# RWKV-7 chunk outputs: products with the state first and together, products with R in a row, one PSUM clear per half

## The chip, the cores and the metric

The kernel runs on one core of one Trainium2 chip. The metric is the device time of one execution in microseconds, as a median over runs. The engines are TensorE (PE, matrix products; PEld is its weight load), VectorE (DVE), ScalarE (ACT), GpSimd (POOL) and SyncE (SP, which issues most of the transfers). Each engine works through its own instruction stream in order and waits for the others by semaphores.

## What is computed

One step of a one-layer decoder over 1024 prompt tokens and 8 x 4 sample tokens: a norm, one input projection, two groups of token mixers (8 RWKV-7 heads of 64, 4 HGRN2 heads of 128), one output projection, a squared-ReLU MLP and a final norm. The change is in the RWKV part, whose reference is a scan over the tokens:

```python
def step(s, inp):
    r_t, w_t, k_t, v_t, kk_t, a_t = inp
    sa = jnp.einsum('bhvk,bhk->bhv', s, -kk_t)
    s = (s * w_t[:, :, None, :] + sa[..., None] * (kk_t * a_t)[:, :, None, :]
         + v_t[..., None] * k_t[:, :, None, :])
    o = jnp.einsum('bhvk,bhk->bhv', s, r_t)
    return s, o
```

Each head has a state s of 64 x 64. The output o of a token comes from the state ahead of a chunk of tokens and from what the tokens of the chunk itself have added.

## The kernel before

The kernel has two stages. In the first, `mixers`, TensorE runs the input projection (`gemm`, lines L208 to L210, three fp32r products of 128 x 128 weights with 256 columns each, `ps_in`) quarter by quarter of the tokens, and between its products the small products of HGRN2, of RWKV, and of the adaLN conditioning (L240, L241, `ps_adp`). The second stage is the output projection and the MLP (`ps_g`, L1137).

RWKV takes the prompt in 8 groups of 128 tokens, each group in two chunks of 64, so 16 chunks one behind another; the samples are a group of their own with their own function. `rwkv_chain` does the chunks. The eight heads lie as four pairs j; the half h of a pair lies on partitions 0 to 63 or 64 to 127 (`hs`). A chunk goes through these steps, with `st` the state ahead of the chunk:

- `ps_U` (L928): for each half four products of `ar` with the state, 64 rows by 64 columns; VectorE adds W (L929).
- `ps_SA` (L933): eight products of the inverse XT with U, 64 by 64; ScalarE copies the result into R (L934).
- `ps_S` (L940): eight products of `btm` with R over 128 rows, halves in turn; VectorE makes the new state of it (L946, L947).
- `ps_O`: for each j and half one product of `ar` with the state (L953, 64 rows) and one of `Ar` with R (L954, 128 rows), both into the same columns of one PSUM tile. ScalarE copies it (L963 in `rwkv_centre`), and VectorE takes the mean and the variance.

The first chunk has no state and leaves out `ps_U` and L953. An fp32 product stands as two records in the trace, so eight products are 16 records. The tag of `ps_O` has one PSUM buffer, which it shares with `ps_oT`, the transposed output of a finished group.

The order on each engine isn't that of the code: a planner with a time model orders the instructions by their dependencies and by the priority in which the generators in `mixers` give them out. So one edit here can move instructions of other functions.

Of the kernel before, what the change touches and what calls it, by code (L numbers as in the profile page):

```python
# [7 lines left out]
F32 = mybir.dt.float32  # L8
# [6 lines left out]
P = 128  # L15
# [68 lines left out]
PT = "maso"  # L84
# [71 lines left out]
class Kernel:  # L156
# [751 lines left out]
    def rwkv_chain(self, g, pool, pp):  # L908

        nc = self.nc  # L910
        V, G, S = nc.vector, nc.gpsimd, nc.scalar
        g["oc"] = pool.tile([P, g["nch"], 4, 64], F32, tag="oc", name="oc", bufs=B_oc)
        g["var"] = pool.tile([P, g["nch"], 4], F32, tag="var", name="var", bufs=B_var)
        W, XT, ar = g["W"], g["XT"], g["ar"]
        for c in range(g["nch"]):
            st = self.rst
            hb = 1 - (c & 1)
            bs = slice(hb * 64, hb * 64 + 64)
            Ar, bt, R = g["Ar"][c], g["bt_"][c], g["R"][c]
            if st is None:  # L920
                U = W
            else:
                U = pool.tile([P, 2, 4, 64], F32, tag="U", name="U", bufs=B_U)
                for h in range(2):
                    hs = slice(h * 64, h * 64 + 64)
                    ps = pp.tile([P, 4, 64], F32, tag=PT[2], name="ps_U")
                    for j in range(4):
                        nc.tensor.matmul(ps[bs, j, :], lhsT=ar[hs, j, c, 0, :], rhs=st[hs, j, :], start=True, stop=True)  # L928
                    V.tensor_tensor(U[bs, h], ps[bs], W[bs, h], op=ALU.add)  # L929
            ps = pp.tile([P, 4, 2, 64], F32, tag=PT[2], name="ps_SA")  # L930
            for h in range(2):
                for j in range(4):
                    nc.tensor.matmul(ps[bs, j, h, :], lhsT=XT[bs, h * 4 + j, :], rhs=U[bs, h, j, :], start=True, stop=True)  # L933
            S.activation(R[bs], ps[bs], AF.Copy)  # L934
            yield
            ps = pp.tile([P, 4, 64], F32, tag=PT[2], name="ps_S")
            for j in range(4):
                for h in range(2):
                    hs = slice(h * 64, h * 64 + 64)
                    nc.tensor.matmul(ps[hs, j, :], lhsT=bt[:, j, hs], rhs=R[:, j, h, :], start=True, stop=True)  # L940
            sn = pool.tile([P, 4, 64], F32, tag="st", name="st", bufs=B_st)
            ptb = g["pt"][:, :, c:c + 1].to_broadcast([P, 4, 64])
            if st is None:
                V.tensor_tensor(sn, ps, ptb, op=ALU.mult)
            else:
                V.tensor_tensor(sn, ps, st, op=ALU.add)  # L946
                V.tensor_tensor(sn, sn, ptb, op=ALU.mult)  # L947
            ps = pp.tile([P, 4, 64], F32, tag=PT[3], name="ps_O")
            for j in range(4):
                for h in range(2):  # L950
                    hs = slice(h * 64, h * 64 + 64)
                    if st is not None:
                        nc.tensor.matmul(ps[hs, j, :], lhsT=ar[hs, j, c, 1, :], rhs=st[hs, j, :], start=True, stop=False)  # L953
                    nc.tensor.matmul(ps[hs, j, :], lhsT=Ar[:, h, j, :], rhs=R[:, j, h, :], start=st is None, stop=True)  # L954
            self.rwkv_centre(pool, g, c, ps)
            self.rst = sn
            yield

# [910 lines left out]
```

## Time and profile before

| | |
|---|---|
| median of 3 runs | 1934.76 us (1928.95 to 1952.22) |
| profiled execution | 1959.38 us |
| its span | 1957.6 us |
| TensorE busy | 1793.7 us, 92% |
| VectorE busy | 1175.9 us, 60% |
| GpSimd busy | 994.3 us, 51% |
| ScalarE busy | 919.0 us, 47% |

The profiled execution is 24.6 us longer than the median. Times within the span are counted from its start. A row of the timeline gives start, length, engine, line, operation, output and inputs, shapes and the number of records; records of one kind behind one another are merged into a row. A matmul's length runs to its modelled end, so that consecutive matmuls overlap, and what one costs is read from start to start. The granted clock of TensorE has two levels in these rows, 1.00 (2.4 GHz) and 0.50 (1.2 GHz).

### The profile page before, as it was taken

How to read it: one execution, taken by the hardware profiler on the slowest of the kernel's cores; microseconds unless marked ns; L12 is line 12 of the kernel's file. 1: busy time of each engine (PE TensorE's matmuls, PEld its weight loads, DVE VectorE, ACT ScalarE, POOL GpSimd, SP SyncE). 2: the span in 40 equal slices, each digit the busy share in tenths (PEclk: the TensorE clock that was granted, in tenths of full speed). 3: DMA queues.
4: the chain of work that ended last, by engine and by line, in shares of the span. 5: the costliest groups of instructions: out<-in, count | busy, mean ns of one | idle time of the engine just before them, and what ended most of it. 6: DMA issues, size and time to landing. Idle time of an engine off the chain costs nothing. (4 is left out here: it accounts for less than half of the span.)

```text
span 1957.6 us, 38042 instructions
## 1 busy us (share of the span) xinstructions
PE 1793.7 (92%) x13988; PEld 1646.0 (84%) x13988; DVE 1175.9 (60%) x2286; ACT 919.0 (47%) x1915; POOL 994.3 (51%) x1418
## 2 busy tenths in 40 slices
PE   6889889899899999999999799699999999999795
PEld 3778778767788888888888799699999899999795
DVE  7676834534744534565544456853333768799998
ACT  5455343653534455555463454545455454333332
POOL 4766362363617233336263566764544637264564
PEclk9998899867679878888796899899999999999896
DMA  7876578645558775635352743353333431423022
GB/s 264 280 235 192 174 237 262 196 125 138 146 154 262 232 230 157 195 117 175 114 160 64 250 170 104 107 167 117 98 99 125 145 132 53 136 75 127 19 76 89
DMA packets 219593, 303.33 MB, mean 155 GB/s; under 512 B 48616, under 2 KB 111464, under 8 KB 216336
## 3 DMA queue, kind: packets, MB, share of 16 engines
q1 hardware_dynamic: 199232, 275.74, 44.6%
q10 hardware_dynamic: 20080, 25.11, 3.8%
q8 instruction: 110, 1.80, 0.4%
q14 instruction: 75, 0.61, 0.1%
q0 software_dynamic: 96, 0.07, 0.0%
HBM read 237.17 MB, written 61.44 MB: 153 GB/s over the span
## 5 line engine op out<-in xcount | busy, mean ns | idle before, releaser
L1137 PE MATMUL ps_g<-bh,whi 128*128 128x264 f32 x1792 | 377.6, 291 | 51.1 <-DVE acc L1449 15.6
L1137 PE MATMUL ps_g<-bh,wlo 128*128 128x264 f32 x1792 | 374.3, 290 | 3.2 <-DVE wlo L1126 3.2
L1137 PE MATMUL ps_g<-bl,whi 128*128 128x264 f32 x1792 | 376.3, 290 | 0.7 <-DVE bl L1426 0.6
L1137 PEld LDWEIGHTS ps_g<-bh,whi 128*128 128x128 f32 x1792 | 287.7, 193 | 55.2 <-ACT whi L1125 16.3
L210 PE MATMUL ps_in<-h,wlo 128*128 128x256 f32 (+1 forms) x960 | 299.0, 313 | 10.0 <-POOL wlo L199 5.6
L208 PE MATMUL ps_in<-h,whi 128*128 128x256 f32 (+1 forms) x960 | 301.1, 318 | 5.7 <-ACT h L1090 3.5
L209 PE MATMUL ps_in<-l,whi 128*128 128x256 f32 (+1 forms) x960 | 298.3, 311 | 3.4 <-DVE l L1091 3.3
L1137 PEld LDWEIGHTS ps_g<-bh,wlo 128*128 128x128 f32 x1792 | 286.0, 193 | 3.8 <-DVE wlo L1126 3.8
L1137 PEld LDWEIGHTS ps_g<-bl,whi 128*128 128x128 f32 x1792 | 287.4, 194 | 1.3 <-DVE bl L1426 1.3
L195 ACT ACTIVATE whi<-wraw 128x512 fp32r<-128x512 f32 x240 | 149.5, 628 | 183.3 <-PE ps_in L209 122.4
L210 PEld LDWEIGHTS ps_in<-h,wlo 128*128 128x128 f32 x960 | 200.1, 209 | 23.1 <-POOL wlo L199 7.9
L208 PEld LDWEIGHTS ps_in<-h,whi 128*128 128x128 f32 x960 | 200.0, 210 | 14.7 <-issue 4.6
L209 PEld LDWEIGHTS ps_in<-l,whi 128*128 128x128 f32 x960 | 200.9, 209 | 10.1 <-DVE l L1091 4.3
L1125 ACT ACTIVATE whi<-wd 128x512 fp32r<-128x512 f32 x112 | 70.1, 630 | 184.2 <-PE ps_g L1137 152.8
L238 POOL TENSOR_TENSOR walo<-wada,wahi 128x256 fp32r<-128x256 f32 x128 | 95.9, 762 | 97.6 <-ACT wahi L237 88.3
L1126 POOL TENSOR_TENSOR wlo<-wu,whi 128x512 fp32r<-128x512 f32 x64 | 90.2, 1412 | 83.4 <-ACT whi L1125 83.2
L1125 ACT ACTIVATE whi<-wu 128x512 fp32r<-128x512 f32 x112 | 69.3, 628 | 119.6 <-PE ps_g L1137 111.0
L1426 POOL TENSOR_TENSOR bl<-u,bh 128x528 fp32r<-128x528 f32 x34 | 63.1, 1862 | 87.9 <-ACT bh L1425 77.8
L862 POOL TENSOR_TENSOR itmp<-ixt,iat 128x60 f32<-128x60 f32 (+24 forms) x248 | 76.1, 307 | 36.0 <-DMA iat<-at_d 17.6
L1426 DVE TENSOR_TENSOR bl<-u,bh 128x528 fp32r<-128x528 f32 x78 | 88.5, 1163 | 5.4 <-ACT bh L1425 5.3
L1126 DVE TENSOR_TENSOR wlo<-wd,whi 128x512 fp32r<-128x512 f32 x91 | 82.7, 913 | 12.3 <-ACT whi L1125 12.3
L864 POOL TENSOR_TENSOR ixt<-ixt,itmp 128x60 f32<-128x60 f32 (+24 forms) x248 | 78.1, 315 | 15.3
(426 smaller groups left out, 3910.7 us busy)
## 6 DMA issues: line engine op xcount, KB each, us to landing
wraw<-w_in SPq DMA_DIRECT2D x240, 256.0 KB, 4.1
wlo<-wlo_d SPq DMA_DIRECT2D x180, 256.0 KB, 3.9
wu<-w_up SPq DMA_DIRECT2D x74, 256.0 KB, 3.0
u<-u_d SPq DMA_DIRECT2D x16, 1056.0 KB, 4.9
wada<-w_ada SPq DMA_DIRECT2D x64, 256.0 KB, 3.8
wd<-w_down SPq DMA_DIRECT2D x64, 256.0 KB, 2.7
wlo_d<-wlo SPq DMA_DIRECT2D x60, 256.0 KB, 3.3
u_d<-c SPq DMA_DIRECT2D x48, 264.0 KB, 3.4
```

Source lines behind the costliest of these rows:

```text
L195: nc.scalar.activation(hi, raw, AF.Copy)
L208: nc.tensor.matmul(out, lhsT=wh, rhs=ah, start=first and k == 0, stop=False)
L209: nc.tensor.matmul(out, lhsT=wh, rhs=al, start=False, stop=False)
L210: nc.tensor.matmul(out, lhsT=wl, rhs=ah, start=False, stop=last and k == len(w) - 1)
L238: (nc.vector if k in ADV else nc.gpsimd).tensor_tensor(lo, raw[:, :, k, :], hi.bitcast(F32), op=ALU.subtract)
L862: G.tensor_tensor(tm, xt[:, 0:ns, j:j + 1].to_broadcast([P, ns, w]), at[:, j, j + 1:32].unsqueeze(1).to_broadcast([P, ns, w]), op=ALU.mult)
L864: G.tensor_tensor(dst, dst, tm, op=ALU.add)
L1125: self.nc.scalar.activation(hi, src, AF.Copy)
L1126: eng.tensor_tensor(lo, src, hi.bitcast(F32), op=ALU.subtract)
L1137: nc.tensor.matmul(out[c], lhsT=w[x][:, k, :], rhs=a[y][:, k, c * 264:c * 264 + 264], start=first and k == 0 and j == 0, stop=last and k = ...
L1426: F().tensor_tensor(lo[:, k, :], src[:, k, :], hi[:, k, :].bitcast(F32), op=ALU.subtract)
```

## The change

The tile of `ps_O` is taken before `ps_SA`, and the eight products with the state are written there in a row, j by j with the halves in turn. The eight products with R follow `ps_S` in a row. Before, each product with the state began a sum of its own (start set) and the one with R closed it. Now only the first product of each half (j = 0) has start set, which clears that half of the PSUM bank; the other products add or overwrite. The number of products, their operands and their shapes are unchanged. `ps_U` and `ps_S` only get another form of loop.

```diff
+        halves = (slice(0, 64), slice(64, 128))
...
+            po = pp.tile([P, 4, 64], F32, tag=PT[3], name="ps_O")
+            if st is not None:
+                for j in range(4):
+                    for hs in halves:
+                        nc.tensor.matmul(po[hs, j, :], lhsT=ar[hs, j, c, 1, :], rhs=st[hs, j, :], start=j == 0, stop=False, skip_group_check=True)
             ps = pp.tile([P, 4, 2, 64], F32, tag=PT[2], name="ps_SA")
...
-            ps = pp.tile([P, 4, 64], F32, tag=PT[3], name="ps_O")
             for j in range(4):
-                for h in range(2):
-                    hs = slice(h * 64, h * 64 + 64)
-                    if st is not None:
-                        nc.tensor.matmul(ps[hs, j, :], lhsT=ar[hs, j, c, 1, :], rhs=st[hs, j, :], start=True, stop=False)
-                    nc.tensor.matmul(ps[hs, j, :], lhsT=Ar[:, h, j, :], rhs=R[:, j, h, :], start=st is None, stop=True)
-            self.rwkv_centre(pool, g, c, ps)
+                for h, hs in enumerate(halves):
+                    nc.tensor.matmul(po[hs, j, :], lhsT=Ar[:, h, j, :], rhs=R[:, j, h, :], start=st is None and j == 0, stop=j == 3, skip_group_check=True)
+            self.rwkv_centre(pool, g, c, po)
```

On TensorE, at the first half of `ps_U` in the second chunk, there stood before one product with the state ahead of the projection:

```order
L904 MATMUL ps_x_3569<-XT,xt_3400 32x32 x8
L928 MATMUL ps_U<-st,ar 64x64 x4
L953 MATMUL ps_O<-st,ar 64x64
L210 MATMUL ps_in<-h_3482,wlo 128x256
L208 MATMUL ps_in<-h_3484,whi 128x256
```

Now all eight stand there (L935 is the new line of the product with the state):

```order
L904 MATMUL ps_x_3569<-XT,xt_3400 32x32 x8
L928 MATMUL ps_U<-st,ar 64x64 x4
L935 MATMUL ps_O<-st,ar 64x64 x8
L210 MATMUL ps_in<-h_3482,wlo 128x256
L208 MATMUL ps_in<-h_3484,whi 128x256
```

At the end of the same chunk on TensorE, products with R and with the state alternated; the rows go on in this way to the eighth product with R:

```order
L241 MATMUL ps_adp<-walo,c_hl 9x256
L940 MATMUL ps_S<-R,btm 64x64 x8
L954 MATMUL ps_O<-R,Ar 64x64
L953 MATMUL ps_O<-st,ar 64x64
L954 MATMUL ps_O<-R,Ar 64x64
```

Now the eight products with R (new line L955) follow those of `ps_S` (now L945), which have the same shape:

```order
L240 MATMUL ps_adp<-wahi,c_hl 18x256
L945 MATMUL ps_S<-R,btm 64x64 x8
L955 MATMUL ps_O<-R,Ar 64x64 x8
L793 MATMUL ps_A<-ar,bk 128x128 x4
L241 MATMUL ps_adp<-walo,c_hl 9x256
```

Of the 15 chunks with a state, eleven now have the eight products with the state in one piece; the others have them in two to eight pieces. In the stream of TensorE two neighbours differ in shape (rows or columns of the array used) 860 times before and 691 times now; of these 257 and 68 have a product of `ps_O` as one of the two. On all engines the instructions ahead of the second chunk and those of the second stage stand as before.

## Rows read from the trace of the kernel before

**Rows 1.** The page: TensorE busy and its granted clock, tenths in 40 slices.

```profile
PE   6889889899899999999999799699999999999795
PEclk9998899867679878888796899899999999999896
```

**Rows 2.** Busy time by engine in seven stretches, 440 to 1090 us: their sum.

```profile
sum 650.00, PE 624.04 PEld 541.25 DVE 323.36 ACT 314.13 POOL 279.01; mean PE 89.15 PEld 77.32 DVE 46.19 ACT 44.88 POOL 39.86
```

**Rows 3.** Groups of TensorE, 440 to 1090 us: busy us, mean ns, idle before.

```profile
L954 PE MATMUL ps_O<-R,Ar 128*64 128x64 f32 x256 | 42.3, 257 | 0.0
L953 PE MATMUL ps_O<-st,ar 64*64 64x64 f32 x240 | 42.0, 259 | 0.9 <-DVE hss L508 0.9
```

**Rows 4.** Timeline of TensorE, second chunk: start us, length us, instruction, records.

```profile
453.49 0.28 PE L953 MATMUL ps_O<-st,ar 64*64 64x64 f32 x2
453.70 0.39 PE L210 MATMUL ps_in<-h,wlo 128*128 128x256 f32 x1
...
465.94 0.28 PE L954 MATMUL ps_O<-R,Ar 128*64 128x64 f32 x2
466.15 0.33 PE L953 MATMUL ps_O<-st,ar 64*64 64x64 f32 x2
...
469.74 1.68 PE L793 MATMUL ps_A<-ar,bk 64*128 64x128 f32 x8
```

**Rows 5.** Timeline of TensorE, a chunk at half clock.

```profile
1035.04 1.96 PE L933 MATMUL ps_SA<-U,XT 64*64 64x64 f32 x16
1036.93 1.11 PE L467 MATMUL ps_l<-hz 128*128 128x64 f32 x4
...
1040.43 1.12 PE L940 MATMUL ps_S<-R,btm 128*64 128x64 f32 x16
1041.34 0.42 PE L954 MATMUL ps_O<-R,Ar 128*64 128x64 f32 x2
...
1047.33 1.06 PE L896 MATMUL ps_x<-ident,XT 32*32 32x32 f32 x16
```

**Rows 6.** Timeline of TensorE: the first chunk's rows, and a ps_SA at full clock.

```profile
450.29 0.69 PE L940 MATMUL ps_S<-R,btm 128*64 128x64 f32 x16
450.80 0.64 PE L954 MATMUL ps_O<-R,Ar 128*64 128x64 f32 x16
451.37 1.06 PE L577 MATMUL ps_os<-hs,hqs 128*32 128x128 f32 x8
...
1015.18 1.14 PE L933 MATMUL ps_SA<-U,XT 64*64 64x64 f32 x16
1016.25 0.49 PE L497 MATMUL ps_o<-hst,hqe 128*128 128x128 f32 x2
```

**Rows 7.** Busy time by stretch: nine at half clock behind alternations, first, last, sum.

```profile
470.20:497.50 27.30, 24.07 (x116) 19.96 (x115) 18.96 (x61) 6.46 (x17) 10.04 (x26) 0.50 0.59 161
...
1071.00:1077.70 6.70, 6.70 (x40) 5.32 (x41) 1.85 (x5) 2.25 (x6) 1.70 (x3) 0.50 0.01 2
sum 139.10, PE 135.88 PEld 116.76 DVE 67.80 ACT 47.10 POOL 36.25; mean PE 15.10 PEld 12.97 DVE 7.53 ACT 5.23 POOL 4.03
```

Behind the stretch stand its length, the busy time of PE, PEld, DVE, ACT and POOL with their instructions, the granted clock, the DMA share and GB/s.

**Rows 8.** The same view of two other stretches.

```profile
569.20:627.20 58.00, 58.00 (x548) 48.95 (x546) 25.61 (x59) 27.20 (x66) 37.95 (x95) 1.00 0.83 258
...
716.00:746.60 30.60, 30.20 (x192) 25.05 (x193) 11.85 (x28) 12.32 (x25) 19.65 (x50) 0.50 0.34 104
```

**Rows 9.** Timeline of TensorE: the projection at full clock and at half clock.

```profile
454.04 0.28 PE L209 MATMUL ps_in<-l,whi 128*128 128x256 f32 x1
454.16 0.28 PE L210 MATMUL ps_in<-h,wlo 128*128 128x256 f32 x1
...
883.51 0.42 PE L208 MATMUL ps_in<-h,whi 128*128 128x256 f32 x1
883.72 0.41 PE L209 MATMUL ps_in<-l,whi 128*128 128x256 f32 x1
```

**Rows 10.** Waits, 440 to 1090 us: us in total, times, longest.

```profile
ACT o L963 <- PE ps_O L954: 43.3, 13, 7.4
```

More of the change, by code (lines that the diff above doesn't have):

```diff
@@ L937, in rwkv_chain @@
             for j in range(4):
-                for h in range(2):
-                    hs = slice(h * 64, h * 64 + 64)
+                for h, hs in enumerate(halves):
                     nc.tensor.matmul(ps[hs, j, :], lhsT=bt[:, j, hs], rhs=R[:, j, h, :], start=True, stop=True)
@@ L947, in rwkv_chain @@
                 V.tensor_tensor(sn, sn, ptb, op=ALU.mult)
-            ps = pp.tile([P, 4, 64], F32, tag=PT[3], name="ps_O")
             for j in range(4):
-                for h in range(2):
-                    hs = slice(h * 64, h * 64 + 64)
-                    if st is not None:
-                        nc.tensor.matmul(ps[hs, j, :], lhsT=ar[hs, j, c, 1, :], rhs=st[hs, j, :], start=True, stop=False)
-                    nc.tensor.matmul(ps[hs, j, :], lhsT=Ar[:, h, j, :], rhs=R[:, j, h, :], start=st is None, stop=True)
-            self.rwkv_centre(pool, g, c, ps)
+                for h, hs in enumerate(halves):
+                    nc.tensor.matmul(po[hs, j, :], lhsT=Ar[:, h, j, :], rhs=R[:, j, h, :], start=st is None and j == 0, stop=j == 3, skip_group_check=True)
+            self.rwkv_centre(pool, g, c, po)
             self.rst = sn
```

## Prediction

> **What bounds the kernel now.** I read the page's busy slices first, then the stretch in which the edited lines run, then TensorE's instructions in order of time, and last the granted clock around them. TensorE is busy in nearly every slice of the span and its clock is below full in many slices of the middle [rows 1]. The edited lines run between about 451 and 1083 us. There the stretches of 440 to 1090 us give TensorE 624.04 us of 650.00, 96%; VectorE has 323.36, ScalarE 314.13, GpSimd 279.01 [rows 2]. So in this stage the in-order instruction stream of TensorE sets the pace: what it no longer does ends the stage earlier, until another engine's waits appear. Before 451 us and after some 1095 us the instructions and their order are the same in both kernels, so nothing is forecast there.
>
> In that stage the two lines of the output product, L953 and L954, take 42.0 and 42.3 us by their groups for 240 and 256 records, 64 columns each [rows 3]. The groups count an instruction to its modelled end, so the overlap is in it; starts are the better measure. Each product is two records in the trace. In a chunk at full clock the products alternate, R, state, R, state: 15 pairs from 465.94 to 469.74, when the next matmul starts, 3.80 us, 0.253 us a pair; one more state pair stood alone earlier, from 453.49 to 453.70, 0.21 us [rows 4]. That is 4.01 us for the chunk. The first chunk has no state and so the eight products with R in a row: from 450.80 to 451.37, 0.57 us for 16 records [rows 6]. The same eight products thus cost far more when products of another shape (64 rows instead of 128) stand between them. At half clock the 15 pairs go from 1041.34 to 1047.33, 5.99 us [rows 5]; with the lone pair, taken at its full-clock 0.21, that is 6.2 us.
>
> **The change part by part.**
>
> *The products with R in a row.* 16 records each in 15 chunks. Price: the first chunk's row, 0.57 us at full clock [rows 6]; at half clock the row of line L940, the same shape and the same alternation of halves, from 1040.43 to 1041.34, 0.91 us [rows 5].
>
> *The products with the state in a row, alternating halves.* 16 records of 64 rows by 64 columns in each of 15 chunks. No row of this kind is in the trace: the two halves use different rows of the array and different output partitions. Bounds: from below the row of L940, which alternates output halves only, 450.29 to 450.80, 0.51 us [rows 6], 0.91 at half clock [rows 5]. From above the present pair, as if each step between halves cost what the change of shape costs now: 8 pairs of 0.253 us, 2.03 us; at half clock 5.99 us / 15 = 0.40 a pair, 3.20 us. Between them stands line L933, the same 64 by 64 shape in a row on one tile, without any overlap: 1015.18 to 1016.25, 1.07 us for 16 records [rows 6], and 1035.04 to 1036.93, 1.89 us, at half clock [rows 5]. I take that: same shape, and it assumes nothing of the halves.
>
> *Sum.* A chunk costs 1.07 + 0.57 = 1.64 us at full clock instead of 4.01, saving 2.37; at half clock 1.89 + 0.91 = 2.80 instead of 6.2, saving 3.40. Of the 15 stretches two run wholly at half clock, the one shown and one before it; the others I count at full clock. 13 x 2.37 + 2 x 3.40 = 37.6 us. With the lower price of the state row: 13 x 2.93 + 2 x 4.38 = 46.9 us. With the upper: 13 x 1.41 + 2 x 2.09 = 22.5 us.
>
> The Trainium skill has a rule against the new state row: on the page TensorEngine Tiling (Array Packing), section Restrictions and Gotchas, different row tiles write to different PSUM banks and cannot use the same bank at the same time. Both halves write one bank here. By that rule there is no overlap between halves, which the L933 price already assumes; if keeping them apart costs more, the sum goes to the 22.5 us of the upper price. No row of before shows which.
>
> *The clock.* In this stage the clock often falls, and many falls come in or right after an alternating stretch: behind the one that ends at 469.74 us [rows 4] the granted clock is 0.50 from 470.20 to 497.50. Nine such half-clock stretches begin in an alternation or within a microsecond of its end, 139.10 us together, TensorE busy for 135.88 of them [rows 7] (a tenth, at the end of the stage, is mostly waiting and isn't counted). At half clock a 256-column matmul starts every 0.21 us, at full clock every 0.12 [rows 9], so a microsecond of such work at half clock would take 0.57: if all nine went away, 139 x 0.43 = 60 us. Not all will: 716.00 to 746.60 us, for instance, is at half clock with no alternation right ahead of it [rows 8], and thin rows of L928, L933 and L940 stay. I take a third, 20 us, as an estimate; the range takes nothing and all.
>
> *One clear per half, and the PSUM bank.* The start flag is a bit of a matmul that is issued anyway; no instruction is added (TensorE issues as many matmuls as before). The one buffer of ps_O is taken earlier in the program, but the first state product stood behind ps_U before as well (453.49 us, [rows 4]), so its waits for the bank are paid already. Seven more products now stand ahead of ps_SA: 1.07 less the 0.21 of the lone pair, 0.86 us a chunk at full clock on the way from ps_U to the new state; as TensorE's stream is the limit, that is in the sum and not beside it.
>
> *Moved work.* The planner places other instructions anew between 451 and 1090 us. Away from ps_O, neighbours of different shape on TensorE rise from 603 to 623. A change of shape costs at most half of a pair less a record's 0.067 us (1.07 / 16): 0.06 to 0.12 us, 20 of them 2 us. Beside that nothing large moves.
>
> *What is late next.* 37.6 + 20 - 2 = 56 us less on TensorE is 9% of its busy time here. ScalarE, which waited 43.3 us for L954 at its copy L963 [rows 10], gets free earlier, but chains through ScalarE, VectorE and GpSimd show more often when their cover is shorter. I take 10% of the gain for that: 50 us. The profiled execution took 1959.38 us, 24.6 above the 1934.76 median, so 1909 us by its own time, and 1885 us beside the median.
>
> **The rivals.**
>
> (a) *More clock comes back.* All nine stretches go and the state row overlaps: 46.9 + 60 - 2 = 105, less 10%, 94 us: 1840 us. For it: 569.20 to 627.20 us, with an alternation in its last microseconds only, is at full clock throughout [rows 8]. Against: half-clock stretches without alternation exist. Chance 0.15.
>
> (b) *The state row does not overlap and pays for each step between halves*, 22.5 us and the third of the clock: 22.5 + 20 - 2 less 10%, 36 us: 1898 us. The skill's rule above would be its reason; the row of L940 speaks against it, but its halves share all rows. Chance 0.13.
>
> (c) *TensorE's gain is taken by others.* The stage waits for the chain of chunks (U, ps_SA, R, ps_S, new state) and for weights, and TensorE idles where it was busy. 0 to 15 us are left: about 1928 us. For it: the edited row isn't on the way to the new state. Against: TensorE's 26 idle us in 650. Chance 0.17.
>
> (d) *Slower, by the clock.* Now ps_U and the state row, 1.6 us of 64-column work, stand together, at the R row ps_S and ps_O another 1.1. Should each of the 15 state rows start a half-clock stretch of its own of the commonest length, some 6.7 us, 15 x 6.7 x 0.43 = 43 us are lost against 37.6 gained: 1940 us. It decides from 37.6 / 0.43 = 87 us of additional half clock on. Against: ps_U and a pair end at 453.70 and the projection behind goes on at 0.12 us a matmul [rows 4, 9]; the row of L933 at 1015.18 [rows 6] is followed by full-clock rows too. Chance 0.05, of it 0.03 over 2% slower.
>
> **How the numbers follow.** Forecast 0.50: PE-bound, 38 us and a part of the clock, 1860 to 1908 us, likeliest 1885. About 2%, 39 us, is what a measurement of this kernel can tell from no change: faster means under 1896. That takes 0.40 of the forecast's 0.50, all of (a) and 0.06 of (b): 0.61. Slower 0.03, the rest 0.36. The range from 1845 to 1925 leaves out the faster half of (a), half of (c) and (d), about 0.2.
>
> **What would show it.** L955 and L935 in the profile after: 16 records of R in about 0.57 us; a state row between 0.5 and 2.0 us, near 1.07. Their groups, 84.3 us together now, fall below half. Half clock in the stage shrinks from nine stretches behind ps_O by some 45 us. The stage still has TensorE busy for over 93%; the first ps_g of the next stage starts some 50 us earlier. Wrong if: the state row takes over 2 us (rival b), TensorE's idle time in the stage rises by tens of microseconds (c), or half clock grows (d).

## The result and the profile after

The changed kernel takes 1872.7 us (median of four runs, 1866.9 to 1885.4) beside 1940.3 us of the kernel before: a ratio of 0.966, with a 95% interval of 0.958 to 0.974. Measured twice more, the ratio was 0.963 (0.957 to 0.970) and 0.968 (0.964 to 0.971). The forecast was 1885 us, within 1845 to 1925, and stood beside the 1934.76 us of three runs; a fourth run of the kernel before moved its median to 1940.3. The gain is 68 us where 50 were forecast.

The page of the changed kernel, TensorE busy and its granted clock in 40 slices, answers to [rows 1]:

```profile
PE   6889789899799999999997996999999899999785
PEclk8998899887799898999988998999999999999896
```

TensorE is nearly as busy as before, but between slices 9 and 21 the clock stays at 8 and 9, apart from two slices at 7, where it stood at 6 to 8 in many slices. The next two rows show the whole stage, from 450 us to the first product of the output projection, first of the kernel before, then of the changed kernel (columns as at [rows 7]; the granted clock is the third number from the end):

```profile
450.00:1095.10 645.10, 614.28 (x5007) 532.96 (x5003) 324.49 (x922) 312.90 (x728) 279.17 (x656) 0.81 0.55 166
```

```profile
450.00:1007.90 557.90, 518.90 (x4964) 456.65 (x4961) 320.61 (x921) 313.49 (x728) 280.26 (x654) 0.91 0.63 192
```

The stage is 87.2 us shorter, the busy times of VectorE, ScalarE and GpSimd change by 4 us at most, and TensorE is 95.4 us less busy, 93% of the stage after 95%. A mean clock of 0.81 means that (1 - 0.81) / 0.5 = 38% of 645.1 us, 245 us, were at half clock; after it is 18% of 557.9, 100 us. (The profiled execution of before was 1959.4 us, 19 above its median of 1940.3, that of the changed kernel at its median; so the traces differ by more than the medians do.)

The groups of the two lines on TensorE, 440 to 1010 us, answer to [rows 3]:

```profile
L935 PE MATMUL ps_O<-st,ar 64*64 64x64 f32 x240 | 14.8, 238 | 2.9 <-DVE bot L1048 2.9
...
L955 PE MATMUL ps_O<-R,Ar 128*64 128x64 f32 x256 | 12.4, 230 | 0.0
```

The same 496 records fall from 84.3 to 27.2 us. The timeline answers to [rows 4] for the second chunk, and shows a state row further on that stands alone:

```profile
463.76 0.69 PE L945 MATMUL ps_S<-R,btm 128*64 128x64 f32 x16
464.28 0.64 PE L955 MATMUL ps_O<-R,Ar 128*64 128x64 f32 x16
464.85 1.16 PE L793 MATMUL ps_A<-ar,bk 64*128 64x128 f32 x8
...
921.51 0.68 PE L935 MATMUL ps_O<-st,ar 64*64 64x64 f32 x16
922.12 1.05 PE L756 MATMUL ps_bo<-cs,rkb 128*128 128x128 f32 x7
```

The R row takes 464.28 to 464.85, 0.57 us, the state row 0.61 us, 1.18 together where a chunk took 4.01. A row's time runs to the start of the next matmul, which here has another shape each time. One row in this trace shows what that is worth: the R row at 834.15 is followed by a matmul of its own shape and takes 0.47 us instead of 0.57, so a change of shape costs 0.10 us:

```profile
834.15 0.64 PE L955 MATMUL ps_O<-R,Ar 128*64 128x64 f32 x16
834.62 0.40 PE L460 MATMUL ps_l<-hz 128*64 128x64 f32 x4
```

And behind the R row of the second chunk the clock does not fall, as it did at 470.20 in [rows 7]; the stretch behind it reads

```profile
464.00:478.00 14.00, 12.02 (x117) 9.38 (x113) 11.77 (x36) 9.84 (x21) 5.02 (x7) 1.00 0.72 218
```

with a granted clock of 1.00. The wait of ScalarE's copy for the last product of a chunk, 43.3 us in [rows 10], is down to a third:

```profile
ACT o L964 <- PE ps_O L955: 14.3, 11, 2.9
```

### The profile page after: what moved, and what is told of

Same layout as the page of the kernel before. It is cut to its first block, busy times and chain, and to the rows that moved or that the text cites. A ratio compares the mean times of both kernels' runs of the same rounds, so it can differ in the third digit from the quotient of the medians.

```text
span 1870.4 us, 38030 instructions
## 1 busy us (share of the span) xinstructions
PE 1699.7 (91%) x13988; PEld 1571.1 (84%) x13988; DVE 1170.3 (63%) x2286; ACT 921.1 (49%) x1917; POOL 997.8 (53%) x1418
## 3 DMA queue, kind: packets, MB, share of 16 engines
q1 hardware_dynamic: 199232, 275.74, 46.7%
## 5 line engine op out<-in xcount | busy, mean ns | idle before, releaser
L210 PE MATMUL ps_in<-h,wlo 128*128 128x256 f32 (+1 forms) x960 | 295.2, 309 | 9.4 <-POOL wlo L199 5.2
L208 PE MATMUL ps_in<-h,whi 128*128 128x256 f32 (+1 forms) x960 | 295.7, 312 | 3.2 <-ACT whi L195 1.2
L209 PE MATMUL ps_in<-l,whi 128*128 128x256 f32 (+1 forms) x960 | 292.4, 305 | 3.7 <-DVE l L1092 3.7
L210 PEld LDWEIGHTS ps_in<-h,wlo 128*128 128x128 f32 x960 | 195.2, 204 | 22.9 <-POOL wlo L199 7.3
L208 PEld LDWEIGHTS ps_in<-h,whi 128*128 128x128 f32 x960 | 194.6, 205 | 11.5 <-issue 4.2
L209 PEld LDWEIGHTS ps_in<-l,whi 128*128 128x128 f32 x960 | 196.3, 205 | 9.4 <-DVE l L1092 4.3
```

The lines of the kernel that those rows point to most:

```text
L208: nc.tensor.matmul(out, lhsT=wh, rhs=ah, start=first and k == 0, stop=False)
L209: nc.tensor.matmul(out, lhsT=wh, rhs=al, start=False, stop=False)
L210: nc.tensor.matmul(out, lhsT=wl, rhs=ah, start=False, stop=last and k == len(w) - 1)
```

## The experiments

Two things had to be told apart. What makes an alternating product dear: the change of shape between 64 and 128 rows (theory A), or adding onto columns that the neighbour has just written (B)? And is the gain the time on TensorE alone (D), or half-clock time behind it as well (C)? Ratios are against the kernel before, measured beside each. The forecast called the two records of one product a pair; in the experiments I count products.

### The old order, with one shape

```diff
-nc.tensor.matmul(ps[hs, j, :], lhsT=ar[hs, j, c, 1, :], rhs=st[hs, j, :], start=True, stop=False)
+nc.tensor.matmul(ps[hs, j, :], lhsT=ar[:, j, c, 1, :], rhs=st[:, j, :], start=True, stop=False)
```

> The order of the kernel before, products with the state and with R in turn into the same columns, but the product with the state runs over all 128 rows, so that both have one shape (its sum then holds the other half's product as well, so the outputs of RWKV differ). Theory A (change of shape between 64 and 128 rows): the pair costs 0.07 us like two products of ps_S instead of 0.253, a chunk 1.1 us instead of 4.0, and the time falls to the changed kernel's: 1865 to 1885 us. Rival B (a product that adds onto columns just written waits for them): pairs stay near 0.25 us and the time near 1940 us.

Measured: 1886.4 us, 0.976 (0.968 to 0.983). The 15 products of the second chunk, R and state in turn into the same columns as before, on TensorE:

```profile
463.74 0.22 PE L954 MATMUL ps_O<-R,Ar 128*64 128x64 f32 x1
463.74 0.22 PE L953 MATMUL ps_O<-st,ar 128*64 128x64 f32 x1
...
464.56 0.28 PE L954 MATMUL ps_O<-R,Ar 128*64 128x64 f32 x2
464.77 1.16 PE L793 MATMUL ps_A<-ar,bk 64*128 64x128 f32 x8
```

From 463.74 to 464.77, 1.03 us for 15 products, 0.069 each instead of 0.253. The order is the old one, each sum has its own clear, state and R still meet in the same columns; only the shape is one. Theory A holds and B falls: the time lies 1 us above the range of A and more than 50 below that of B.

### Alternation without the same columns

```diff
+seq = [(j, h) for j in range(4) for h in range(2)]
...
+def with_state(i):
+    j, h = seq[i]
+    hs = halves[h]
+    nc.tensor.matmul(po[hs, j, :], lhsT=ar[hs, j, c, 1, :], rhs=st[hs, j, :], start=j == 0, stop=False, skip_group_check=True)
...
+if st is not None:
+    with_state(0)
+for i, (j, h) in enumerate(seq):
+    if st is not None and i < 7:
+        with_state(i + 1)
+    nc.tensor.matmul(po[halves[h], j, :], lhsT=Ar[:, h, j, :], rhs=R[:, j, h, :], start=st is None and j == 0, stop=j == 3, skip_group_check=True)
```

> One clear per half as in the changed kernel, but the products with the state and with R alternate again, shifted by one: the product with R follows the state's product for the next half and never adds onto the columns that its neighbour has written. Theory A (change of shape): pairs near 0.25 us again, 7 of them in a row, 1925 to 1945 us. Rival B (adding onto columns just written): pairs fall to 0.07 to 0.13 us, 1870 to 1890 us.

Measured: 1933.7 us, 0.997 (0.992 to 1.003): no difference from the kernel before can be seen. On TensorE:

```profile
465.58 0.33 PE L961 MATMUL ps_O<-R,Ar 128*64 128x64 f32 x2
465.84 0.33 PE L954 MATMUL ps_O<-st,ar 64*64 64x64 f32 x2
466.10 0.33 PE L961 MATMUL ps_O<-R,Ar 128*64 128x64 f32 x2
```

0.26 us a product again, with one clear per half as in the changed kernel and no product on the columns of its neighbour. So the clear gains nothing by itself. The rows need it to stand apart: with a start at every product with the state, as in the next experiment, the outputs lack part of those products.

### A clear with every product

```diff
-start=j == 0
+start=True
```

> The changed kernel with the start flag on every product with the state instead of on the first of each half (the products with R then overwrite most of them, so that the outputs lack part of the products with the state). Theory: the flag costs nothing, 1865 to 1885 us, the state row near 0.6 us. Rival F (a clear costs time): the row grows by six more clears, the time by 5 us or more.

Measured: 1881.9 us, 0.971 (0.966 to 0.975), against 1877.5 us, 0.968 (0.964 to 0.971), of the changed kernel. The intervals overlap, and the state row that answers to the one at 921.51 takes 924.33 to 924.94, the same 0.61 us:

```profile
924.33 0.68 PE L935 MATMUL ps_O<-st,ar 64*64 64x64 f32 x16
924.94 1.16 PE L756 MATMUL ps_bo<-cs,rkb 128*128 128x128 f32 x8
```

The flag costs nothing that shows.

### The halves one after the other

```diff
-for j in range(4):
-    for hs in halves:
+for hs in halves:
+    for j in range(4):
```

> As the changed kernel, but the eight products with the state run through one half and then through the other, so that neighbours use the same rows of the array. Theory A (the gain is the change of shape that is gone; the alternating halves only overlap a little more): the state row takes 1.07 us like ps_SA instead of the 0.67 us measured in the changed kernel (451.74 to 452.41), so 15 x 0.4 = 6 us are lost: 1879 us against 1873. Rival H (the alternation of the halves is the main gain): 1900 us or more, the row near 2 us.

Measured: 1886.1 us, 0.975 (0.966 to 0.984). The state row:

```profile
450.81 0.91 PE L935 MATMUL ps_O<-st,ar 64*64 64x64 f32 x16
451.66 0.39 PE L210 MATMUL ps_in<-h,wlo 128*128 128x256 f32 x1
```

0.85 us instead of 0.61 with alternating halves. Record by record, the alternating row at 921.51 starts two records, one of each half, every 0.058 us, the second 0.006 to 0.007 behind the first; this row starts one record in the same 0.058 us, except where its halves meet. So neighbours from different halves overlap, though both write one PSUM bank, each in partitions of its own. That is 15 x 0.24 = 4 us; the measured time doesn't separate this kernel from the changed one. Rival H, that the alternation of halves is the main gain, falls.

### The state row late

```diff
-nc.tensor.matmul(ps[hs, j, :], lhsT=bt[:, j, hs], rhs=R[:, j, h, :], start=True, stop=True)
+last = nc.tensor.matmul(ps[hs, j, :], lhsT=bt[:, j, hs], rhs=R[:, j, h, :], start=True, stop=True)
...
+with self.tc.issue_after(last.ins):
+    for j in range(4):
+        for hs in halves:
+            nc.tensor.matmul(po[hs, j, :], lhsT=ar[hs, j, c, 1, :], rhs=st[hs, j, :], start=j == 0, stop=False, skip_group_check=True)
```

> As the changed kernel, but the state row is held back until the products of ps_S are issued, so that it stands directly ahead of the R row: both rows stay whole, nothing is done early. Theory A (shape changes): two more changes of shape a chunk at most, 15 x 2 x 0.12 = 4 us: 1873 to 1880 us. Rival E (the products with the state gain by being done while the chunk waits for R): a state row of 0.67 us moves onto the path to the output in each chunk and the stage loses 10 us or more: 1885 us and above.

Measured: 1888.1 us, 0.977 (0.970 to 0.984). The second chunk of this kernel:

```profile
471.76 0.69 PE L940 MATMUL ps_S<-R,btm 128*64 128x64 f32 x16
472.38 0.68 PE L953 MATMUL ps_O<-st,ar 64*64 64x64 f32 x16
472.99 0.69 PE L956 MATMUL ps_O<-R,Ar 128*64 128x64 f32 x16
```

The state row takes the same 0.61 us, and ps_S ahead of it 0.62 instead of 0.52, R behind it 0.61 (to 473.60) instead of 0.57. ps_S has 0.1 us more, as a change of shape at its end costs. The rows are as theory A has them, but the time lies in the range of rival E. The stage is 577.3 us long with TensorE busy for 531.1 (46 idle, after 39), its clock 0.89. Most of the gain is there with the row late. Standing early may be worth some of it, up to 1% by these medians, but the intervals overlap, and this isn't settled.

### TensorE's time put back, dense

```diff
+for _ in range(6):
+    nc.tensor.matmul(po.rearrange("p j v -> p (j v)"), lhsT=self.ident, rhs=Ar.rearrange("p h j v -> p (h j v)")[:, 0:256], start=True, stop=True, skip_group_check=True)
```

> The changed kernel with about as much TensorE time put back as the change took away, but as dense work: ahead of each state row six products of 128 x 128 by 256 columns into the same tile, overwritten after (a product of 512 columns took 1.05 us in the kernel before, 457.89 to 458.94, so six of 256 about 2.6 to 3 us a chunk, 40 to 45 us in all). Theory C (the alternation cost its own time and, beyond that, half-clock time behind it): the time rises by 30 to 45 us only, to 1905 to 1920, and half clock between 450 us and the next stage stays near the changed kernel's 102 us. Rival D (only the time on TensorE counts): the same time as with the thin filler that runs beside it.

Measured: 1899.5 us, 0.978 (0.972 to 0.984), 28 us over the changed kernel beside it (1871.5), a little under the range of theory C. The six products take 452.02 to 454.81, 2.8 us, in a chunk; from start to start over all chunks they take 46.7 us.

### TensorE's time put back, thin

```diff
+for i in range(10):
+    j, h = i // 2 % 4, i % 2
+    hs = halves[h]
+    nc.tensor.matmul(po[hs, j, :], lhsT=ar[hs, j, c, 1, :], rhs=st[hs, j, :], start=True, stop=True, skip_group_check=True)
+    nc.tensor.matmul(po[hs, j, :], lhsT=Ar[:, h, j, :], rhs=Ar[:, h, j, :], start=True, stop=True, skip_group_check=True)
```

> The changed kernel with about as much TensorE time put back, as thin work: ahead of each state row ten pairs that alternate between 64 and 128 rows, overwritten after (0.253 us a pair before, 2.5 us a chunk, 38 us in all). Theory C (alternation also draws the clock down): half clock rises by 50 us or more over the changed kernel's 102 us, and the time to 1925 to 1950 us, 15 to 30 us above the dense filler's. Rival D (only the time on TensorE counts): 1905 to 1920 us, as the dense filler's.

Measured: 1991.1 us, 1.026 (1.019 to 1.033). But this put back twice what I had meant: a loop issues two products, 20 in all, each of them 0.257 us, 5.1 us a chunk at full clock. As a comparison of like with like it is no good, so it was cut to six loops, 12 products, 3.1 us:

> The thin filler again, cut to the dense filler's size: 12 products a chunk alternating between 64 and 128 rows. A product in an alternation took 0.257 us in the thin filler at full clock (448.75 to 449.00), so 12 take 3.1 us a chunk, 46 us in all, as the dense filler's six (46.7 us). Theory C (alternation also draws the clock down): half clock between 450 us and the next stage rises to 150 us or more (dense filler 91) and the time lies 20 us or more above the dense filler's 1899, 1920 to 1945 us. Rival D (only the time on TensorE counts): 1895 to 1910 us.

Measured: 1948.1 us, 1.004 (1.001 to 1.007), 71 us over the changed kernel beside it (1877.5), where the dense filler cost 28. The stage of both, dense first:

```profile
450.00:1034.00 584.00, 561.80 (x5144) 485.44 (x5142) 314.37 (x921) 315.46 (x725) 274.39 (x649) 0.92 0.60 181
```

```profile
450.00:1077.40 627.40, 605.10 (x5272) 515.93 (x5271) 315.23 (x912) 311.54 (x720) 268.57 (x643) 0.84 0.56 168
```

TensorE is 96% busy in both. With dense work 8% of 584.0 / 0.5 = 93 us are at half clock, with thin work 16% of 627.4 / 0.5 = 201 us. The fillers themselves take 46.7 us (dense) and 54.3 (thin), from start to start, so about 8 of the 43 us between 28 and 71 are their own. The rest goes with 108 us more of half clock, worth 46 at most by the forecast's 0.43 us a microsecond. In every one of the runs the clock of the thin filler's kernel was lower, too: 0.892 to 0.906 over the whole run against 0.923 to 0.928. Theory C holds, D falls.

How the thin work brings the clock down is shown less well. One fall comes in the middle of a filler, where the step from start to start goes from 0.25 to 0.41 us:

```profile
449.06 0.33 PE L936 MATMUL ps_O<-st,ar 64*64 64x64 f32 x2
449.31 0.48 PE L937 MATMUL ps_O<-Ar 128*64 128x64 f32 x2
449.72 0.47 PE L936 MATMUL ps_O<-st,ar 64*64 64x64 f32 x2
```

But of the 14 falls from this one to the end of the stage only four come in a filler or within a microsecond behind one (none of 11 with the dense filler). And the two fillers differ in the size of their products as well as in the alternation; which of the two the clock answers to isn't separated here.

The dense filler also shows that the changed kernel has slack: of its 47 us only 28 come through, and TensorE's idle time in the stage falls from 39 us to 22.

### ps_U and the state row together

```diff
+po = pp.tile([P, 4, 64], F32, tag=PT[3], name="ps_O")
...
+os = halves[1 - h]
 for j in range(4):
     nc.tensor.matmul(ps[bs, j, :], lhsT=ar[hs, j, c, 0, :], rhs=st[hs, j, :], start=True, stop=True)
+    nc.tensor.matmul(po[os, j, :], lhsT=ar[os, j, c, 1, :], rhs=st[os, j, :], start=j == 0, stop=False, skip_group_check=True)
```

> The changed kernel with each half's four products of ps_U alternating with the four products with the state of the other half: other rows of the array and another PSUM bank, so each pair could overlap as the halves of the state row do. If they overlap, ps_U hides in the state row: up to 15 x 0.5 = 7 us faster than the changed kernel, 1866 us against 1873. If the planner draws them apart or they don't overlap: 1870 to 1885 us.

Measured: 1862.1 us, 0.960 (0.951 to 0.968), beside 1871.5. Once more with more runs, and the changed kernel beside it:

> The kernel with ps_U paired with the state products of the other half once more, more rounds beside the changed kernel: if its gain of 9 us over the changed kernel (1862.1 against 1871.5) is real, 1858 to 1868 us; if it was the spread of the runs, 1868 to 1878.

> The changed kernel beside it with as many rounds: 1868 to 1878 us.

Measured: 1861.1 us, 0.959 (0.956 to 0.963), and 1877.5 us, 0.968 (0.964 to 0.971). The intervals don't touch: this kernel is faster than the changed one by 16 us or 0.9%, more than the 7 us expected of the overlap, and not by the records' own time. Where the planner kept the order, ps_U does overlap:

```profile
451.51 0.27 PE L930 MATMUL ps_U<-st,ar 64*64 64x64 f32 x1
451.52 0.27 PE L931 MATMUL ps_O<-st,ar 64*64 64x64 f32 x1
...
451.97 0.68 PE L931 MATMUL ps_O<-st,ar 64*64 64x64 f32 x9
452.58 0.39 PE L210 MATMUL ps_in<-h,wlo 128*128 128x256 f32 x1
```

Eight records of ps_U and seven of the state row take 0.46 us together, but behind them the planner puts the rest of the state row with its products in one half: 451.97 to 452.58, 0.61 us for nine records. Summed from each record's start to the next record's over ps_U and ps_O, without idle time, 43.0 us here stand against 44.0 in the changed kernel beside it. What is less is TensorE's idle time in the stage, 31 against 38 us, and half clock:

```profile
450.00:1001.00 551.00, 520.28 (x4964) 457.14 (x4964) 323.22 (x921) 317.75 (x728) 277.12 (x651) 0.91 0.63 192
```

```profile
450.00:1018.70 568.70, 531.09 (x5015) 466.51 (x5014) 321.46 (x922) 314.18 (x730) 279.47 (x659) 0.89 0.62 188
```

The first row is this kernel, the second the changed kernel. Half clock is 99 against 125 us in this pair of traces, but the changed kernel alone has 100, 123 and 125 in its three traces, where its idle time is 38 or 39 us in each. Over the six runs of each kernel the median clock of the whole run is 0.925 against 0.918, so some of the half clock is real. Whether the pairing does this or the planner's other order that came with it stays open.

The repeat of the changed kernel beside the fillers, their base:

> The changed kernel once more, on the same chip as the fillers, as their base: 1865 to 1885 us by both theories, half clock near 102 us between 450 us and the next stage.

Measured: 1871.5 us.

## Why the prediction was right, step by step

- **TensorE bounds the stage.** Right. TensorE lost 95 us of busy time and the stage 87; the other engines' work stayed, and what their waits took back is the 8 us more of idle time (31 to 39 us). The 10% taken for that, 6 us, was about the right size. TensorE is still busy for 93% of the stage, just at the sign that the forecast had set.
- **The price of the alternation is the change of shape.** Right. It was read from 0.57 us for a row without alternation against 0.253 us a product with it [rows 4, 6]; the same-shape and the shifted experiment settle it. The 0.06 to 0.12 us that the forecast gave for a single change hold the 0.10 measured.
- **The R row, 0.57 us.** Exact.
- **The state row, 1.07 us by L933.** Mis-sized: 0.61 us. The lower bound, 0.51 us by L940, was the nearer, since the halves overlap. That is 15 x 0.46 = 7 us more gain. The sum of starts over all 496 records, without idle time, falls from 66.8 to 23.2 us, 43.6 us, where the step had 37.6, with 22.5 and 46.9 as its ends. Even one half after the other takes only 0.85 us: where its halves meet, three records start 0.004 to 0.006 us behind their neighbours instead of 0.058, while L933 stays on one half throughout.
- **The skill's rule on PSUM banks, rival (b).** The Trainium skill's page TensorEngine Tiling (Array Packing), section Restrictions and Gotchas, says that different row tiles write to different banks and can't access one bank at the same time. Here the measurement differs: with both halves in one bank, but in partitions of their own, the row is faster with alternating halves (0.61 us) than without (0.85 us). Rival (b) falls.
- **The clock.** Right in kind and too small. A third of the nine stretches was taken, some 45 us less of half clock for 20 us. The trace of the changed kernel has 145 us less (245 to 100), more than the 139 of all nine. Of the stage's 87.2 us, 43.6 are the records' own and 8 were lost to idle time, so about 52 remain for the clock and whatever else the new order moved; by the forecast's 0.43 us a microsecond, 145 us give 62 at most. In the medians the share is smaller. Over all runs of the last comparison the clock of the whole run has a median of 0.899 before (17 runs) and 0.918 after (six), which is some 390 and 310 us at half clock: 80 us less, 34 us at most. With 43.6 for the records and 8 off for idle time that makes 70 us, where these runs differ by 62. So the clock gave some 26 to 34 us in the medians, where 20 were forecast. Taking a third was a guess between nothing and all, which no row of before picked; that it came near is luck. The fillers show that alternating thin work costs clock in this stage.
- **The bank taken early, and the start flag.** Right: TensorE waits for L1048, which reads the bank's last user, 2.9 us in all, and the flag costs nothing that shows. The 2 us for moved work can't be told apart.
- **Rivals (a), (c) and (d).** (a) had the right direction in both of its parts, a state row near its lower price and more clock, but its 1840 us lies 33 below what was measured. (c) falls with the length of the stage. (d), a fall of the clock at each new row, falls too: half clock shrank.

## What to carry to other kernels

Put products of one shape of the array, rows by columns, in a row; let them alternate only between tiles of that same shape, and give the accumulation one clear per half if this is what it takes. Read a product's cost from start to start in the timeline, not from the length of its record: a product's 0.253 against 0.07 us here was hidden in mean record lengths of 0.26 and 0.23 to 0.24. When thin alternating work stands in a stage bound by TensorE, look at the granted clock of the whole stage, too: the thin filler cost 43 us more than the dense one, and only about 8 of them were its own. All of this was measured with fp32 products of 64 columns.

## What was not expected

A TensorE stream that hardly ever waits can have its clock halved: both fillers left TensorE 96% busy, and half clock was 93 us with dense and 201 us with alternating thin work of nearly the same length. And two tiles on different halves of the rows, writing to different partitions of one PSUM bank, overlap: 0.61 us for 16 records against 0.85.
